# Two layers of a hybrid trunk on one core: ends of mixer branches moved behind the next projection, the softmax scaled by pairs of heads on VectorE, low priority for filler work only inside the triangular inverse

## The chip, the cores and the metric

One core of a Trainium2 chip runs one program. The metric is its device time in microseconds (us), median of several runs. The engines of the core have a queue of instructions each and work through it strictly in order: TensorE (PE in the profile; its weight loads are shown apart as PEld), VectorE (DVE), ScalarE (ACT) and GpSimd (POOL). SyncE (SP) issues the transfers of weights. An instruction waits on semaphores until the tiles that it reads are written and the tile that it overwrites is free.

## The reference

Two layers, 256 tokens, width 1024, in f32. Each layer adds the sum of four token mixers to its input and normalises, then does the same with a mixture of experts. What matters here, cut short:

```python
proj = x @ w_proj                                 # one wide input projection
y_a = _mla_branch(...)     # low-rank attention, 8 heads, causal softmax
y_b = _gla_branch(...)     # gated linear attention, chunks of 64
y_c = _gdn_branch(...)     # gated delta rule: conv of 4 taps on q, k, v, chunked, triangular solve
y_d = _rwkv7_branch(...)   # RWKV-7 state update
# attention inside _mla_branch:
s = jnp.where(key_pos[None, :] <= q_pos[:, None], s, -jnp.inf)
p = jax.nn.softmax(s, axis=-1)
o = einsum('bhqk,bkhd->bqhd', p, v)
# end of _gla_branch and of _gdn_branch, per head of 128 channels:
o = _rmsnorm(o, norm_g) * jax.nn.silu(gate)
# merge and output projection:
merged = sum(sigmoid(gate_logits[:, :, n]) * (y_n @ w_branch[n]) for n in range(4))
mix = merged @ w_out
x = _layernorm(alpha * x + mix)
x = _layernorm(alpha * x + moe(x))                # 16 experts, top 2
```

## The kernel before

All weights are streamed: a load brings 512 KB as a tile `raw` (128x1024, f32), ScalarE rounds it to a high half `hi` (L285, `split_hi`) and VectorE subtracts to get the low half `lo` (L289, `split_lo`). Each product is then three matmuls (Xh by hi, Xl by hi, Xh by lo). One call of `proj(i)` makes 256 columns of the input projection for all 256 tokens in a PSUM bank tagged "pp": two loads, 48 matmuls of 128x128 by 128x256. The banks have three tags: "pp" (two banks) for projections, "pc" (four) and "pf" (two) for the work inside the branches.

The four branches are written one after the other, and each interleaves its own chain (transposes, small matmuls, VectorE and ScalarE work) with the calls of `proj` for its inputs. A scheduler orders the instructions of each engine when the program is built; code that is written earlier or has a higher priority is taken first. While a branch works on a chain without projections of its own, `gap(us)` issues some microseconds of filler work: pieces of `merge(n, y)`, which project a finished branch and its gate. Fillers run at a low priority (`tc.high_priority(offset=-LOW)`), and the next matmul of the branch is put behind the last of them.

The places that the change touches:

- Attention in the MLA branch handles two groups of four heads (`hg`). For each, ScalarE makes eight exponentials (L914, L916: for each head a block `me0` of 128 queries by 128 keys and a block `me1` of 128 by 256), with the row sums in `sms`. VectorE takes the reciprocal of all sums (L918), GpSimd multiplies `me0` (L919) and `me1` (L920), and TensorE transposes them (by a multiplication with the constant `ident`, shown as `con`) for the product with v.
- `headnorm_T` ends both the gated linear attention (`gla`) and the delta rule (`gdn`): squares, sums, a power of -0.5 on GpSimd (`rsqrt`, L632), the product `hon` (L962), and a function `post()` that transposes `hon` on TensorE and multiplies by the gate into `y`. `gla` calls both its `post()` after a `gap`; `gdn` calls that of the second chunk after a `gap`.
- `gdn` convolves q, k and v on VectorE into `gacc` (L992, L1010); for v four transposes of `gacc` follow at once. In its chunk step, `gr` is scaled on VectorE (L1099) and subtracted from v on GpSimd (L1100).
- The output projection makes two halves (`hf`) of the columns in two banks tagged "pp" each. The last two banks of that tag were those of `merge_last`, emptied into `gth` (L626). `out_mm` (L1549 to L1551) multiplies the merged tile `mg`.

`rLT` is a tile of the RWKV branch that GpSimd sets to zero ahead of use (L1390).

## Time and profile before

| what | value |
|---|---|
| median of 3 runs | 1575.59 us (1574.55 to 1580.73) |
| profiled execution, its own time | 1570.59 us |
| span of its instructions | 1568.7 us |
| mean granted TensorE clock | 0.969 |
| TensorE busy | 1444.0 us, 92% |
| VectorE busy | 1147.0 us, 73% |
| ScalarE busy | 878.3 us, 56% |
| GpSimd busy | 178.6 us, 11% |

The span runs from the first to the last instruction; 1.9 us of the execution's time lie outside of it. The profiled execution is one run, and 5.0 us faster than the median of the others. Busy shares are averages over stages: the mixers of the two layers lie at 20 to 475 and 795 to 1255 us, the experts at 485 to 775 and 1265 to 1555 us.

### The profile page before, as it was taken

The page shows a single profiled execution, that of the slowest core. Times are in us where ns is not written, and L with a number is a line of the kernel's source. Part 1 is how long each engine was busy: PE and PEld are TensorE (multiplying, and loading weights), DVE is VectorE, ACT ScalarE, POOL GpSimd, SP SyncE. Part 2 cuts the span into 40 slices and gives each one's busy share as a digit, 9 for nine tenths or more (in the row PEclk, how much of TensorE's full clock was granted, in tenths as well). Part 3 has the DMA queues.
Part 4 walks back from the last instruction along what each step waited for, and adds up shares of the span by engine and source line. Part 5 has one row for each costly group of instructions (what it writes and reads, how often), then busy time and mean ns, then how long its engine had stood idle before and what let it go on. Part 6 is the DMA issues. An engine that isn't in the chain of part 4 may idle for free. (4 is left out here: it accounts for less than half of the span.)

```text
span 1568.7 us, 26671 instructions
## 1 busy us (share of the span) xinstructions
PE 1444.0 (92%) x10266; PEld 1155.3 (74%) x10266; DVE 1147.0 (73%) x1843; ACT 878.3 (56%) x1379; POOL 178.6 (11%) x203
## 2 busy tenths in 40 slices
PE   6999999899996999999789999997999979999995
PEld 6789989799985656654378899896999756665552
DVE  5567768883668988879656577678745689888795
ACT  4445445444347878776453563453333488787762
POOL 2111103211200000000011111232211000000000
PEclk8999999999998999999989999998999989999998
DMA  5434444363555899999633345343636468999992
GB/s 203 138 104 135 139 142 130 114 201 116 202 178 218 308 329 361 356 342 363 220 116 121 115 149 155 98 155 92 185 123 227 149 243 303 339 353 357 352 367 99
DMA packets 111446, 329.30 MB, mean 210 GB/s; under 512 B 29008, under 2 KB 31824, under 8 KB 111312
## 3 DMA queue, kind: packets, MB, share of 16 engines
q1 hardware_dynamic: 111312, 327.52, 60.4%
q8 instruction: 84, 1.38, 0.3%
q14 instruction: 50, 0.41, 0.1%
HBM read 322.63 MB, written 3.80 MB: 208 GB/s over the span
## 5 line engine op out<-in xcount | busy, mean ns | idle before, releaser
L289 DVE TENSOR_TENSOR lo<-raw,hi 128x1024 fp32r<-128x1024 f32 x476 | 584.5, 1249 | 114.9 <-ACT hi L285 106.7
L285 ACT CAST hi<-raw 128x1024 fp32r<-128x1024 f32 x476 | 486.9, 1047 | 303.0 <-PE pp L498 124.0
L504 PE MATMUL pp<-Xh,hi 128*128 128x256 f32 x736 | 216.4, 294 | 6.7 <-ACT hi L285 4.1
L504 PE MATMUL pp<-Xh,lo 128*128 128x256 f32 x736 | 214.8, 292 | 3.4 <-DVE lo L289 3.3
L504 PE MATMUL pp<-Xl,hi 128*128 128x256 f32 x736 | 213.8, 290 | 0.0
L504 PEld LDWEIGHTS pp<-Xh,hi 128*128 128x128 f32 x736 | 145.3, 197 | 9.8 <-ACT hi L285 4.7
L498 PE MATMUL pp<-Xh,hi 128*128 128x256 f32 x512 | 148.3, 291 | 3.0 <-ACT gth L574 3.0
L2020 PE MATMUL s<-whole,hT 128*64 128x512 f32 x336 | 150.2, 596 | 0.0
L504 PEld LDWEIGHTS pp<-Xh,lo 128*128 128x128 f32 x736 | 145.1, 197 | 4.4 <-DVE lo L289 3.8
L504 PEld LDWEIGHTS pp<-Xl,hi 128*128 128x128 f32 x736 | 145.1, 197 | 0.6 <-issue 0.2
L498 PE MATMUL pp<-Xl,hi 128*128 128x256 f32 x512 | 145.2, 285 | 0.0
L498 PE MATMUL pp<-Xh,lo 128*128 128x256 f32 x512 | 144.6, 284 | 0.0
L2020 PEld LDWEIGHTS s<-whole,hT 128*64 128x64 f32 x336 | 43.7, 137 | 93.5 <-issue 88.4
L1979 PE MATMUL u<-lo,r 128*128 128x512 f32 x256 | 103.1, 403 | 8.3 <-DVE lo L289 8.0
L1979 PE MATMUL g<-lo,r 128*128 128x512 f32 x256 | 102.5, 400 | 3.3 <-DVE lo L289 3.1
L1978 PE MATMUL g<-hi,r 128*128 128x512 f32 x256 | 103.8, 406 | 0.0
L498 PEld LDWEIGHTS pp<-Xh,hi 128*128 128x128 f32 x512 | 97.7, 191 | 6.4 <-ACT gth L574 3.4
L1978 PE MATMUL u<-hi,r 128*128 128x512 f32 x256 | 101.0, 394 | 0.0
L498 PEld LDWEIGHTS pp<-Xl,hi 128*128 128x128 f32 x512 | 97.9, 192 | 0.8 <-issue 0.6
L498 PEld LDWEIGHTS pp<-Xh,lo 128*128 128x128 f32 x512 | 97.9, 192 | 0.7 <-issue 0.6
L2026 ACT CAST Y<-s 64x512 fp32r<-64x512 f32 x60 | 34.8, 580 | 72.6 <-PE s L2020 72.6
L1979 PEld LDWEIGHTS u<-lo,r 128*128 128x128 f32 x256 | 48.0, 188 | 28.6 <-DVE lo L289 19.5
(563 smaller groups left out, 2795.3 us busy)
## 6 DMA issues: line engine op xcount, KB each, us to landing
raw<-win SPq DMA_DIRECT2D x156, 512.0 KB, 3.7
raw<-wg SPq DMA_DIRECT2D x122, 512.0 KB, 7.1
raw<-wu SPq DMA_DIRECT2D x120, 512.0 KB, 5.1
whole<-wd SPq DMA_DIRECT2D x92, 512.0 KB, 7.4
raw<-wd SPq DMA_DIRECT2D x36, 512.0 KB, 6.0
raw<-wbr SPq DMA_DIRECT2D x32, 512.0 KB, 4.0
raw<-wout SPq DMA_DIRECT2D x16, 512.0 KB, 4.7
whole<-wu SPq DMA_DIRECT2D x8, 512.0 KB, 5.1
```

Of the source, the lines that this page charges most:

```text
L285: done["hi"] = S.copy(hi, src).ins
L289: done["lo"] = V.tensor_tensor(lo, src, hi.bitcast(F32), OP.subtract).ins
L498: last[0] = f(*args, **kw).ins
L504: f(*args, **kw)
L1978: PE.matmul(x["p"], xs, hi[:, 512 * k2:512 * (k2 + 1)], start=(k == 0), stop=False)
L1979: PE.matmul(x["p"], xs, lo[:, 512 * k2:512 * (k2 + 1)], start=False, stop=(k == 7))
L2020: PE.matmul(py, x["hT"][:, f - NSP, :], w[:, cs], start=(f == 0), stop=(f == 3))
L2026: S.copy(Y[0:64, cs], py)
```

## The change

Five edits:

1. The softmax's reciprocal and its two multiplications go by pairs of heads, inside the loop that transposes, and the multiplications are done on VectorE.
2. The end of `gla` (both `post()`), the end of `gdn` (the second chunk's `post()`) and the transposes of v in `gdn` are not issued where they were, but put on a list `pending`; `settle()`, called right after the next `proj`, issues them. The `gap`s ahead of both ends are gone.
3. In the delta rule's chunk step VectorE subtracts `gr` instead of GpSimd.
4. The output projection's first half uses two banks tagged "pc".
5. `gap` takes its priority as an argument: fillers are low only in the triangular inverse, and elsewhere have the normal priority.

(`fr` frees a tile's slot.)

```diff
-        def gap(us):
+        def gap(us, low=0):
...
-                    with tc.high_priority(offset=-LOW):
+                    with tc.high_priority(offset=-low):
...
-                gap(GT / len(LTs))
+                gap(GT / len(LTs), LOW)
...
-                V.reciprocal(sm0, sm0)
-                G.tensor_tensor(e0, e0, bcast(sm0[:, 0, :], 128), OP.mult)
-                G.tensor_tensor(e1, e1, bcast(sm0[:, 1, :], T), OP.mult)
                 a0 = al([128, 4, T], "ma0")
                 a1 = al([128, 4, 128], "ma1")
                 for j in range(2):
+                    js = slice(2 * j, 2 * j + 2)
+                    V.reciprocal(sm0[:, :, js], sm0[:, :, js])
+                    V.tensor_tensor(e0[:, js, :], e0[:, js, :], bcast(sm0[:, 0, js], 128), OP.mult)
+                    V.tensor_tensor(e1[:, js, :], e1[:, js, :], bcast(sm0[:, 1, js], T), OP.mult)
                     p = bank(bk).rearrange("p (h k) -> p h k", h=2)
...
                 p = proj(2 + j)
+                settle()
                 pin = al([128, 2, T], "gpin")
...
                     V.scalar_tensor_tensor(acc, th, 1.0, acc, op0=OP.add, op1=OP.mult)
-                    pt = bank(bk).rearrange("p (c a d) -> p c a d", c=2, a=2)
-                    for a in range(2):
-                        for c in range(2):
-                            tp(pt[:, c, a, :], acc[:, a, 128 * c:128 * (c + 1)], ident)
-                    S.activation(vtok[:, :, 2 * g:2 * g + 2, :], pt, AF.Copy, scale=0.5)
+                    fr(th, pin)
+
+                    def turn_v(acc=acc, g=g):
+                        pt = bank(bk).rearrange("p (c a d) -> p c a d", c=2, a=2)
+                        for a in range(2):
+                            for c in range(2):
+                                tp(pt[:, c, a, :], acc[:, a, 128 * c:128 * (c + 1)], ident)
+                        S.activation(vtok[:, :, 2 * g:2 * g + 2, :], pt, AF.Copy, scale=0.5)
+                        fr(acc)
+
+                    pending.append(turn_v)
+                    continue
                 fr(acc, th, pin)
             for j in range(2):
                 p = proj(8 + j)
+                settle()
...
-            G.tensor_tensor(r1, vtok[:, 1], r1, OP.subtract)
+            V.tensor_tensor(r1, vtok[:, 1], r1, OP.subtract)
...
             post1 = headnorm_T(qs, rqk[:, 1, :], 1, gdnnh, zs, y)
-            gap(G4)
-            post1()
-            fr(qs, zs)
+            fr(qs)
+
+            def end():
+                post1()
+                fr(zs)
+
+            pending.append(end)
...
+        pending = []
+
+        def settle():
+            while pending:
+                pending.pop(0)()
...
-            yield 0.0
-            gap(G4)
-            for f in posts:
-                f()
-            fr(E1, E2, vt, og, at, St)
+            fr(E1, E2, at, St)
+
+            def end():
+                for f in posts:
+                    f()
+                fr(vt, og)
+
+            pending.append(end)
...
             p = proj(10)
+            settle()
...
         for hf in range(2):
-            pb = [bank("pp") for _ in range(2)]
+            pb = [bank("pp" if hf else "pc") for _ in range(2)]
```

What the scheduler makes of it on TensorE, at three places.

TensorE at the first pair of the first head group (`pp_...` are projections, `con_63` the identity): before, the two halves of the group start with both `me0`, late in projection `pp_761`.

```order
L504 MATMUL pp_761<-Xh_131,lo_795 128x256
L504 MATMUL pp_761<-Xh_131,hi_794 128x256
L504 MATMUL pc_496<-con_63,me0_480 128x128
L504 MATMUL pc_502<-con_63,me0_480 128x128
L504 MATMUL pp_761<-Xl_132,hi_794 128x256
L504 MATMUL pp_761<-Xh_131,lo_795 128x256
L504 MATMUL pp_761<-Xh_131,hi_794 128x256
L504 MATMUL pp_761<-Xl_132,hi_794 128x256
L504 MATMUL pp_761<-Xh_131,lo_795 128x256
L504 MATMUL pc_496<-con_63,me1_481 128x128
```

The same place after, from the first transpose on (the projection is now numbered `pp_767`).

```order
L504 MATMUL pp_767<-Xh_131,hi_770 128x256
L504 MATMUL pc_496<-con_63,me0_480 128x128
L504 MATMUL pp_767<-Xl_132,hi_770 128x256
L504 MATMUL pp_767<-Xh_131,lo_771 128x256
L504 MATMUL pp_767<-Xh_131,hi_770 128x256
L504 MATMUL pp_767<-Xl_132,hi_770 128x256
L504 MATMUL pc_496<-con_63,me1_481 128x128
L504 MATMUL pc_496<-con_63,me0_480 128x128
L504 MATMUL pc_496<-con_63,me1_481 128x128
L504 MATMUL pp_767<-Xh_131,lo_771 128x256
L504 MATMUL pp_767<-Xh_131,hi_800 128x256
```

The first pair's four transposes stand 18 projection matmuls further ahead than the first did before, and the second pair's follow nine matmuls later.

TensorE at the end of the gated linear attention, before (projection `pp_1105` of the delta rule goes on around it).

```order
L504 MATMUL pp_1105<-Xl_132,hi_1108 128x256
L504 MATMUL pp_1105<-Xh_131,lo_1109 128x256
L504 MATMUL pc_1087<-con_63,hon_1070 128x128 x4
L504 MATMUL pp_1105<-Xh_131,hi_1108 128x256
L504 MATMUL pp_1105<-Xl_132,hi_1108 128x256
```

And after.

```order
L504 MATMUL pp_1099<-Xl_132,hi_1132 128x256
L504 MATMUL pp_1099<-Xh_131,lo_1133 128x256
L504 MATMUL pc_1160<-con_63,hon_1076 128x128 x4
L504 MATMUL pc_1166<-con_63,hon_1091 128x128 x4
L504 MATMUL pp_1195<-Xh_131,hi_1198 128x256
```

Before, the first four stood 3 matmuls into that projection and the second four, not shown, 19 matmuls later; after, both stand at its end, behind all of its matmuls.

TensorE at the output projection of layer 0, before.

```order
L1549 MATMUL pp_5033<-hi_5037,mg_5014 128x512
L1550 MATMUL pp_5033<-lo_5038,mg_5014 128x512
L1549 MATMUL pp_5034<-hi_5037,mg_5014 128x512
L1550 MATMUL pp_5034<-lo_5038,mg_5014 128x512
L1551 MATMUL pp_5033<-hi_5037,mg_5017 128x512
```

And after (`mg_5020` is the same high half as `mg_5014`, `mg_5023` the same low half as `mg_5017`).

```order
L1574 MATMUL pc_5039<-hi_5043,mg_5020 128x512
L1575 MATMUL pc_5039<-lo_5044,mg_5020 128x512
L1574 MATMUL pc_5040<-hi_5043,mg_5020 128x512
L1575 MATMUL pc_5040<-lo_5044,mg_5020 128x512
L1574 MATMUL pp_5139<-hi_5143,mg_5020 128x512
L1574 MATMUL pp_5140<-hi_5143,mg_5020 128x512
L1576 MATMUL pc_5039<-hi_5043,mg_5023 128x512
```

The first half's four matmuls go to two "pc" banks; ahead of the first that needs the low half stand now two of the second half, in the "pp" banks.

## Rows read from the trace of the kernel before

**Rows 1.** Totals of the page: busy us (share of the span) and instructions by engine.

```profile
PE 1444.0 (92%) x10266; PEld 1155.3 (74%) x10266; DVE 1147.0 (73%) x1843; ACT 878.3 (56%) x1379; POOL 178.6 (11%) x203
```

**Rows 2.** TensorE's waits: for which tile; us in total, times, longest.

```profile
PE pc L504 <- DVE hon L962: 7.4, 8, 1.4
PE pc L504 <- POOL me L920: 6.3, 4, 1.8
...
PE pf L504 <- DVE gacc L1010: 5.2, 2, 2.7
...
PE pp L1549 <- DVE gth L626: 4.1, 2, 2.6
...
PE pc L504 <- POOL gr L1100: 1.9, 2, 0.9
...
PE pc L504 <- POOL me L919: 1.5, 4, 0.5
```

**Rows 3.** Windows: mixers, then MoE of layer 0; busy us (x instructions) by engine.

```profile
20.00:475.00 455.00, 430.09 (x3900) 398.76 (x3898) 300.89 (x547) 206.75 (x345) 76.39 (x84) 0.98 0.45 143
485.00:775.00 290.00, 281.74 (x1186) 170.61 (x1185) 245.81 (x305) 218.68 (x323) 7.03 (x9) 0.99 0.90 330
```

**Rows 4.** Timeline, attention's first head group: start us, us, engine, ..., [idle before, releaser].

```profile
69.43 0.21 ACT L916 ACTIVATION_READ_ACCUMULATOR me<-pc,mxs,rq 128x1 f32 x1
...
71.39 0.23 ACT L916 ACTIVATION_READ_ACCUMULATOR me<-pc,mxs,rq 128x1 f32 x1
...
72.58 4.30 DVE L289 TENSOR_TENSOR lo<-raw,hi 128x1024 fp32r<-128x1024 f32 x2 [0.73 <-ACT hi L285]
...
73.03 0.44 PE L504 MATMUL pc<-con,me 128*128 128x128 f32 x2 [0.34 <-POOL me L919]
...
73.66 0.28 PE L504 MATMUL pp<-Xl,hi 128*128 128x256 f32 x1
...
73.78 0.28 PE L504 MATMUL pp<-Xh,lo 128*128 128x256 f32 x1
...
75.86 1.31 PE L504 MATMUL pc<-con,me 128*128 128x128 f32 x10 [1.80 <-POOL me L920]
```

**Rows 5.** Line L920 on its own: durations in ns, min/median/max.

```profile
L920 POOL TENSOR_TENSOR me<-me,sms x4: 1895/2874/2876, 72.9 to 866.7; 128x1024 f32<-128x1024 f32 x4
```

**Rows 6.** VectorE's groups by shape: busy us, mean ns of one.

```profile
L289 DVE TENSOR_TENSOR lo<-raw,hi 128x1024 fp32r<-128x1024 f32 x476 | 584.5, 1249 | 114.9 <-ACT hi L285 106.7 <-PE g L1979 3.3 <-issue 1.4
...
L1459 DVE TENSOR_TENSOR ryt<-pc,rst 128x256 f32<-128x256 f32 x8 | 3.4, 424 | 0.2
...
L918 DVE RECIPROCAL sms<-sms 128x8 f32<-128x8 f32 x4 | 0.8, 204 | 10.7 <-ACT me L916 10.7
```

**Rows 7.** Timeline, end of the gated linear attention.

```profile
115.92 0.66 PE L504 MATMUL pc<-con,hon 128*128 128x128 f32 x4 [1.25 <-DVE hon L962]
...
118.56 0.69 DVE L962 TENSOR_TENSOR hon<-pc,hst 128x512 f32<-128x512 f32 x1 [0.93 <-POOL hst L632]
...
119.40 0.63 PE L504 MATMUL pc<-con,hon 128*128 128x128 f32 x4 [0.56 <-DVE hon L962]
```

**Rows 8.** Timeline of VectorE ahead of gacc.

```profile
154.14 0.17 DVE L1028 TENSOR_SCALAR grq<-gs 128x8 f32<-128x8 f32 x1 [3.10 <-POOL gs L632]
```

**Rows 9.** Delta rule's second chunk: timeline (two rows), memset rLT by line.

```profile
232.92 1.26 POOL L1100 TENSOR_TENSOR gr<-gvt,gr 128x512 f32<-128x512 f32 x1 [2.77 <-DVE hst L955]
...
245.49 0.63 PE L504 MATMUL pc<-con,hon 128*128 128x128 f32 x4 [1.36 <-DVE hon L962]
...
L1390 POOL MEMSET rLT<- 128x1024 f32 x4 | 3.8, 955 | 7.2 <-DVE rBK L1362 4.2 <-DVE rv L1313 1.3 <-DMA raw<-win 1.2
```

**Rows 10.** Timeline of TensorE at the first output projection.

```profile
446.30 0.50 PE L1549 MATMUL pp<-hi,mg 128*128 128x512 f32 x1 [1.54 <-DVE gth L626]
...
447.24 0.39 PE L1549 MATMUL pp<-hi,mg 128*128 128x512 f32 x1
447.47 0.39 PE L1550 MATMUL pp<-lo,mg 128*128 128x512 f32 x1
```

More of the change, by code (lines that the diff above doesn't have):

```diff
@@ L704, in tri_inv @@
                         S.copy(Dl[r, :, r], Dc[r, 0])
-                gap(GT / len(LTs))
+                gap(GT / len(LTs), LOW)
             P1s = []
@@ L715, in tri_inv @@
                 P1s.append(P1)
-                gap(GT / len(LTs))
+                gap(GT / len(LTs), LOW)
             for P1, Dc, Dt, Dl in zip(P1s, Dcs, Dts, Dls):
@@ L728, in tri_inv @@
                 fr(P1, Dc)
-                gap(GT / len(LTs))
+                gap(GT / len(LTs), LOW)
             Q1s = []
@@ L738, in tri_inv @@
                 Q1s.append(Q1)
-                gap(GT / len(LTs))
+                gap(GT / len(LTs), LOW)
             for Q1, Dt in zip(Q1s, Dts):
@@ L745, in tri_inv @@
                 fr(Q1)
-                gap(GT / len(LTs))
+                gap(GT / len(LTs), LOW)
             return Dts
```

## The prediction

> **What bounds the kernel now.** I read the page's totals first. TensorE is busy for 1444.0 us of a span of 1568.7 us [rows 1], so the time can fall only where TensorE stands still, or where its work is slower than it need be. The windows by stage come next: in the mixers of layer 0 TensorE is busy 430.09 of 455 us and in the following MoE 281.74 of 290 us [rows 3]. The MoE is nearly full whenever it starts, so a microsecond saved in the mixers moves everything behind it forward, and since both layers run the same code each saving counts twice. Then I read TensorE's waits, because each names the tile that was late [rows 2]. Six of them are what the edits touch: the head-normalised tile hon 7.4 us in 8 waits, the softmax tiles me 6.3 us in 4 (L920) and 1.5 us in 4 (L919), gacc 5.2 us in 2, the gate tile gth behind which the first output matmuls stand 4.1 us in 2, and gr 1.9 us in 2. Together they are 26.4 us.
>
> A wait's row is a little smaller than what the wait costs. Two matmuls in a stream start 0.12 us apart (73.66 and 73.78) although each is shown for 0.28 us [rows 4]. The transpose that waited for me started at 75.86, that is 2.08 us after the last matmul where 0.12 us would have been normal, so it cost 1.96 us and its row says 1.80. The difference, 0.16 us, is added to each wait. For 22 waits it makes 3.5 us, and the ceiling of all edits is 30 us.
>
> **The change part by part.**
>
> *Softmax scaling.* Now, per group of four heads, VectorE takes one reciprocal when all eight exponentials are done, then GpSimd multiplies me0 (L919) and me1 (L920, mostly 2.87 us [rows 5]), and TensorE waits for both [rows 4]. For four groups the two rows of waits plus 8 times 0.16 make 7.8 + 1.3 = 9.1 us. In the changed order the work goes by pairs: reciprocal (0.20 us), a multiplication of 128x256 and one of 128x512, on VectorE. Rows of those shapes take 0.42 and 0.69 us [rows 6, 7], so a pair costs 1.31 us and a group 2.6 us, where VectorE spent 0.2. The first pair's last exponential ends at 69.64 and the second's at 71.62 [rows 4], so me0 of the first pair is ready near 69.64 + 0.20 + 0.42 = 70.3 and its me1 at 71.0; the second pair's are ready at 72.2 and 72.9. TensorE used to arrive at 73.03 - 0.34 - 0.16 = 72.53 [rows 4], with 18 more matmuls of the projection ahead than now; it will arrive 18 x 0.12 = 2.2 us earlier, at 70.3 to 70.4. Four matmuls further, at 70.9, it needs me1 (a wait of some 0.1 us). Nine matmuls and some transposes after that, near 72.4, it needs the second pair (0.1 to 0.5 us). I leave 0.4 us of waiting in each group, 1.6 us in all: **gain 7.5 us**. The bounds: 9.1 us if no wait stays, about 4 us if each group keeps one wait of 1.3 us, the length of one pair's work.
>
> Those 2.4 us per group are added to a queue that also makes the weights' low halves, so I looked at what VectorE did beside GpSimd. Two of these splits took 4.30 us from 72.58, while L920 ran [rows 4], and one takes 1.25 us on average [rows 6]: GpSimd's multiplication cost VectorE 1.8 us of its own time. VectorE's real addition is therefore 2.4 - 1.8 = 0.6 us per group, and its idle time ahead of the reciprocal covers that. The Trainium skill (Perfetto Trace Analysis, Optimizing Scalar/DVE Operations) warns that shifting work between GpSimd and VectorE might not help, as the two share a read port. The row bears out the sharing: what GpSimd gives up, VectorE gets back. If the port were all that counts, this edit would gain nothing and the sum would be 4.75 us; I hold the order to count, since TensorE waits for me's time of completion and not for VectorE's total, and the scaling by pairs can start 2 us before the last exponential.
>
> *End of the gated linear attention.* The two sets of hon transposes stood 3 and 22 matmuls into a projection; now both stand behind its 39 further matmuls. They waited 1.25 and 0.56 us [rows 7], so 1.41 + 0.72 = 2.13 us with the correction. The second hon was made from 118.56 on in 0.69 us [rows 7], so it is ready near 119.25. TensorE began the second set at 119.40; without the two waits, without the first set's 0.4 us of transposes and with 17 more matmuls ahead it comes to the first set at 119.40 - 2.13 - 0.4 + 17 x 0.12 = 118.9 and to the second at 119.3. Nothing is left of the wait, or 0.1 us of it: **gain 2.1 us a layer, 4.2 us**. What ends later is y, and its consumer is a merge that is only issued much further on.
>
> *Transposes of v in the delta rule.* The diff puts them behind the next projection, but TensorE already ran them there: they stood 9 and 3 matmuls behind it before and the order is unchanged. What is late is gacc, because VectorE's queue is held for 3.10 us at L1028 until GpSimd's power of a 128x16 tile is done [rows 8], and the convolution that makes gacc is queued behind. The changed program has the same instructions in the same order there. **Gain 0**; the other bound is the whole wait, 5.2 + 0.3 = 5.5 us.
>
> *Delta rule, second chunk.* The subtraction that makes gr moves from GpSimd, where it ended at 234.18 after 1.26 us [rows 9], to VectorE at 0.69 us [rows 7]. There a token shift and a small product now stand ahead of it, some 0.4 us by my estimate, so about 0.2 us is won. Against this, in layer 0 the memset of rLT (0.96 us [rows 9]) now waits for that subtraction and stands in GpSimd's queue ahead of the power that the first hon needs; VectorE's L962 waits for the power, and u, hon and a scan are queued behind it. That makes hon some 0.9 us later, and 14 projection matmuls (1.7 us) that now precede it on TensorE about cover this. The second hon, with its wait of 1.36 us [rows 9], is now behind a projection, but only 34 matmuls stand between the two where 43 stood, so TensorE comes 1.1 us earlier to a tile whose chain has one split (1.25 us) in front of it now instead of one in the middle. I take +0.2 us a layer lost, **-0.4 us**. The bounds: 1.52 us lost again per layer (the second wait doubles), or the two waits for hon gone, 2 x 1.1 us net gained.
>
> *Output projection.* The first half's accumulators no longer need the bank that gth (L626) holds up to 446.30 [rows 10]. Four matmuls go ahead in them, but then come the second half's first two, in the old banks, and the second of these waits for the same gth. At 446.30 TensorE resumes as before, and the next after that needs a low half of mg that comes no sooner than before; it is two matmuls further by then, 0.23 us each (447.24 to 447.47 [rows 10]): **gain 0.5 us a layer, 0.95 us**. The bounds are 0 and the whole wait, 4.1 + 0.3 = 4.4 us.
>
> *Priority.* Outside the triangular inverse the filler matmuls have normal priority. In layer 0 TensorE's order isn't changed by it; in layer 1 a few groups of five to twenty-four matmuls change places in the RWKV part. **0**, with 1 us either way.
>
> **The sum.** 7.5 + 4.2 + 0 - 0.4 + 0.95 + 0 = 12.25 us, 0.8%. The profiled execution took 1570.59 us and would take 1558.3. The median of the runs shown is 1575.59 us, 5.0 us more than the profiled one; carried over, the prediction is 1563.3 us.
>
> **Rivals.**
> *All six waits go:* 30 us less, 1546 us. It needs VectorE's hold at L1028 to end, and no row or order shows why it should. 7%. A part of it, the gacc wait alone going, would give 1558.
> *The waits only change their name:* each pair of heads keeps a wait of about 1.3 us, the second hon doubles its wait, the output gains nothing. That is 12.25 - 3.5 - 2.6 - 0.95 = 5 us gained, 1570 us, within what can't be told from no change (0.5% of 1575.59 is 7.9 us, and I take that as the limit of this measurement). For it speaks how small the margins above are (0.1 us at several places), against it that TensorE reaches them behind other work. With the softmax's whole gain lost, as by the Trainium skill's warning above, it would be 1571. 25%.
> *Slower:* VectorE's queue becomes the limit in attention. Its six instructions of a group stand together, so a split of weights behind them can be held from 69.64 to 72.9, 3.3 us. If TensorE needs that split each time, four groups cost 13.2 us instead of gaining 7.5, and the kernel takes 1563.3 + 20.7 = 1584 us. It decides once splits are made less than 3.3 us before use. Against it: the two splits beside L920 ended at 76.88, and TensorE still waited only for me. 10%.
> My forecast, 1557 to 1568 us, has 58%.
>
> **How the numbers follow.** Faster by over 0.5% means under 1567.7 us: nearly all of the forecast, the 7%, and little of the second rival: 0.63. Within 0.5%: 0.28. Slower: 0.09. The range runs from 1554 (all waits of softmax, hon and output gone, or gacc's too) to 1577 us (the second rival with its spread).
>
> **What would show it.** Right: in the profile after, the rows for me and for hon of the gated linear attention are gone or under 0.5 us each; gacc's wait still shows about 2.6 us twice; the output still waits for gth, by the four matmuls' time less; VectorE's busy time grows by less than 10 us and the splits beside the softmax take 1.25 us again. Wrong: a new wait of TensorE for a low half around the attention, a hon wait above 1.5 us in the delta rule, or a new order in layer 1's RWKV part that waits longer than before.

## The result, and the profile after

The changed kernel takes 1559.73 us (median of 4 runs, 1556.61 to 1562.93), the kernel before 1575.07 us beside it (4 runs, 1573.76 to 1580.73). The ratio is 0.9895 with a 95% interval of 0.9867 to 0.9923: about 1.0% faster. The profiled executions took 1570.59 and 1557.93 us, their spans differ by 1568.7 - 1556.0 = 12.7 us; the prediction was 12.25 us for them.

The page's totals after, to be read beside [rows 1]. TensorE has the same instructions; it is busy for 1.3 us less and stands still for 11.4 us less.

```profile
span 1556.0 us, 26689 instructions
...
PE 1442.7 (93%) x10266; PEld 1155.7 (74%) x10266; DVE 1148.4 (74%) x1865; ACT 877.1 (56%) x1379; POOL 159.2 (10%) x193
```

TensorE's waits after (for which tile; us in total, times, longest), beside [rows 2]:

```profile
PE pf L504 <- DVE gacc L1013: 5.2, 2, 2.7
...
PE pc L504 <- DVE hon L964: 4.1, 4, 1.3
...
PE pp L1574 <- DVE gth L627: 1.8, 2, 1.4
...
PE pp L1574 <- ACT hi L285: 1.2, 1, 1.2
...
PE pc L504 <- DVE hst L959: 0.8, 2, 0.4
```

Both rows for me and the row for gr are gone, and hon is down from 8 waits with 7.4 us to 4 with 4.1 us, all of them in the delta rule. The wait for gacc is exactly what it was. The output still waits for gth, 1.8 instead of 4.1 us, and has a new wait beside it, for a high half of weights. In place of gr stands a small one for hst, at the same matmul: 0.42 us in each layer where 0.94 stood.

To see what each stage gained I took the starts of the input projections' matmuls out of the traces (they come in the same number in every kernel) and measured stages between two of them: attention from the 193rd to the 385th, the end of the gated linear attention (GLA) to the 433rd, the transposes of v from the 673rd to the 721st, the delta rule's chunks from the 865th to the 1105th. In layer 1 the stages start at the 2017th, 2257th, 2545th and 2737th and hold the same matmuls, except that attention has 48 more there, ahead of the softmax. In us, worked out so from the traces (layer 0 / layer 1):

| kernel | attention | end of GLA | v | chunks |
|---|---|---|---|---|
| before | 40.97 / 55.05 | 12.84 / 12.84 | 10.36 / 9.09 | 57.08 / 56.70 |
| changed | 35.89 / 51.95 | 10.66 / 10.65 | 10.35 / 10.43 | 56.48 / 56.76 |
| mla_only | 35.88 / 52.06 | 12.84 / 12.84 | 10.19 / 10.58 | 58.97 / 60.34 |
| pool_pairs | 37.54 / 53.20 | 10.66 / 10.65 | 10.39 / 10.59 | 57.02 / 57.64 |
| dve_whole | 35.95 / 51.24 | 10.65 / 10.65 | 10.34 / 9.11 | 57.12 / 57.19 |
| gacc_fix | 35.88 / 51.87 | 10.66 / 10.66 | 6.19 / 6.19 | 57.20 / 55.44 |
| gr_pool | 35.92 / 51.86 | 10.66 / 10.66 | 8.86 / 9.09 | 57.92 / 57.91 |
| gdn_now | 35.92 / 51.90 | 10.66 / 10.66 | 10.33 / 9.09 | 55.73 / 55.79 |

So attention gained 5.1 and 3.1 us, the end of the gated linear attention 2.18 and 2.19, the chunks 0.6 and nothing; the stage of v lost 1.3 us in layer 1. That is 11.8 of the 12.7 us. What lies outside these stages nearly cancels: 1.5 us gained ahead of the first attention and 2.0 us in layer 0 behind the chunks (the output projection apart), against 0.6 and 1.5 us lost in the two output projections and 1.1 us between the chunks and the output projection of layer 1.

The 3.1 us of layer 1 are too small a figure for the softmax. From the 2065th matmul on, the counterpart of layer 0's 193rd, attention took 40.31 us before and 35.73 in the changed kernel, both at full clock: 4.6 us gained. The 48 matmuls ahead of it took 1.5 us longer, with a new wait of 0.4 us (for kh) and 4.0 instead of 1.7 us at TensorE's lower clock.

Part of the scatter is TensorE's clock: a stage in which it was granted the lower of its two levels, 1.2 instead of 2.4 GHz, for 3.4 us is up to 1.7 us longer. In the stage of v it shows best: 8.86 to 9.1 us without such a stretch, 10.2 to 10.6 with one. Both figures of mla_only's chunks hold one too.

The timeline after of the first head group (start us, us, engine, line, ...), VectorE and then TensorE, beside [rows 4]:

```profile
68.17 0.18 DVE L923 RECIPROCAL sms<-sms 128x4 f32<-128x4 f32 x1 [0.41 <-ACT me L917]
68.38 0.43 DVE L924 TENSOR_TENSOR me<-me,sms 128x256 f32<-128x256 f32 x1
68.73 0.68 DVE L925 TENSOR_TENSOR me<-me,sms 128x512 f32<-128x512 f32 x1
70.14 0.18 DVE L923 RECIPROCAL sms<-sms 128x4 f32<-128x4 f32 x1 [0.73 <-ACT me L917]
70.36 0.42 DVE L924 TENSOR_TENSOR me<-me,sms 128x256 f32<-128x256 f32 x1
70.70 0.68 DVE L925 TENSOR_TENSOR me<-me,sms 128x512 f32<-128x512 f32 x1
71.68 1.23 DVE L289 TENSOR_TENSOR lo<-raw,hi 128x1024 fp32r<-128x1024 f32 x1 [0.29 <-ACT hi L285]
...
68.95 0.30 PE L504 MATMUL pc<-con,me 128*128 128x128 f32 x1
...
69.57 0.51 PE L504 MATMUL pc<-con,me 128*128 128x128 f32 x3
...
70.98 0.49 PE L504 MATMUL pc<-con,me 128*128 128x128 f32 x3
```

VectorE takes 0.18, 0.43 and 0.68 us for a pair, close to the prices read from other lines [rows 6, 7]. The last pair's me1 is done at 71.4, 1.3 us after its last exponential, where GpSimd was done 4.2 us after it. None of TensorE's rows carries a wait, and the next split, at 71.68, takes 1.23 us again.

The end of the gated linear attention on TensorE, beside [rows 7]: all eight transposes in one go, with no wait ahead.

```profile
112.26 1.04 PE L504 MATMUL pc<-con,hon 128*128 128x128 f32 x8
```

The second chunk of the delta rule: VectorE's subtraction, GpSimd, TensorE's two sets of transposes, beside [rows 9].

```profile
224.59 0.68 DVE L1111 TENSOR_TENSOR gr<-gvt,gr 128x512 f32<-128x512 f32 x1
...
225.33 0.95 POOL L1415 MEMSET rLT<- 128x1024 f32 x1 [3.82 <-DVE gr L1111]
226.36 1.26 POOL L633 TENSOR_TENSOR hst<-hst,con 128x4 f32<-128x4 f32 x1
...
229.16 0.63 PE L504 MATMUL pc<-con,hon 128*128 128x128 f32 x4 [0.95 <-DVE hon L964]
...
236.81 0.66 PE L504 MATMUL pc<-con,hon 128*128 128x128 f32 x4 [1.17 <-DVE hon L964]
```

The subtraction ends at 225.27, the memset of rLT starts on it and the power only behind the memset, as the prediction had it. The first hon now costs 0.95 us of waiting instead of 0.54, and the second 1.17 instead of 1.36 (layer 1: 0.70 instead of 0.54, 1.27 instead of 1.37).

### The profile page after: what moved, and what is told of

Same layout as the page of the kernel before. It is cut to its first block, busy times and chain, and to the rows that moved or that the text cites. A ratio compares the mean times of both kernels' runs of the same rounds, so it can differ in the third digit from the quotient of the medians.

```text
span 1556.0 us, 26689 instructions
## 1 busy us (share of the span) xinstructions
PE 1442.7 (93%) x10266; PEld 1155.7 (74%) x10266; DVE 1148.4 (74%) x1865; ACT 877.1 (56%) x1379; POOL 159.2 (10%) x193
## 5 line engine op out<-in xcount | busy, mean ns | idle before, releaser
L289 DVE TENSOR_TENSOR lo<-raw,hi 128x1024 fp32r<-128x1024 f32 x476 | 578.7, 1236 | 118.1 <-ACT hi L285 109.6
```

Source lines behind the costliest of these rows:

```text
L289: done["lo"] = V.tensor_tensor(lo, src, hi.bitcast(F32), OP.subtract).ins
```

## The experiments

A ratio to the kernel before is given where a kernel ran several times. The others (out_pp, out_pin, out_fix, out_only, gr_pool, gdn_now) have one execution each, from 1556.6 to 1580.13 us, and of them only stages are compared, as the kernel before took up to 1592.28 us beside them.

**mla_only.** The kernel before with the first edit.

```diff
-                V.reciprocal(sm0, sm0)
-                G.tensor_tensor(e0, e0, bcast(sm0[:, 0, :], 128), OP.mult)
-                G.tensor_tensor(e1, e1, bcast(sm0[:, 1, :], T), OP.mult)
                 for j in range(2):
+                    js = slice(2 * j, 2 * j + 2)
+                    V.reciprocal(sm0[:, :, js], sm0[:, :, js])
+                    V.tensor_tensor(e0[:, js, :], e0[:, js, :], bcast(sm0[:, 0, js], 128), OP.mult)
+                    V.tensor_tensor(e1[:, js, :], e1[:, js, :], bcast(sm0[:, 1, js], T), OP.mult)
```

> The kernel before with edit 1 alone (softmax scaled by pairs on VectorE). Theory: the softmax edit by itself gives two thirds of the whole gain, since the time that matmul progress gained between attention's start and end was 5.1 and 4.9 us in the changed kernel; so 8 to 10 us less than before (ratio near 0.994), no wait for me left in TensorE's rows. Rival, that the shared port decides and shifting work between GpSimd and VectorE gives nothing: within 2 us of before, with new waits for a low half beside the attention.

Ratio 0.9952 (0.9926 to 0.9978), 7.6 us by that (3.5 to 11.7), just under the expected 8 to 10. Attention is as short as in the changed kernel (35.88 and 52.06 us; 35.83 from the 2065th matmul on), 9.6 us less than before in the two layers, and no wait for me is left, so the edit does its whole work alone. The 9 runs lie far apart (1560.95 to 1575.9 us) and go with the mean granted clock (0.971 and 0.959), which makes the ratio the blunter of the two measures.

**pool_pairs and dve_whole.** The changed kernel with one half of the first edit each: pairs, but on GpSimd; VectorE, but the whole group at once.

```diff
-                    V.tensor_tensor(e0[:, js, :], e0[:, js, :], bcast(sm0[:, 0, js], 128), OP.mult)
-                    V.tensor_tensor(e1[:, js, :], e1[:, js, :], bcast(sm0[:, 1, js], T), OP.mult)
+                    G.tensor_tensor(e0[:, js, :], e0[:, js, :], bcast(sm0[:, 0, js], 128), OP.mult)
+                    G.tensor_tensor(e1[:, js, :], e1[:, js, :], bcast(sm0[:, 1, js], T), OP.mult)
...
+                V.reciprocal(sm0, sm0)
+                V.tensor_tensor(e0, e0, bcast(sm0[:, 0, :], 128), OP.mult)
+                V.tensor_tensor(e1, e1, bcast(sm0[:, 1, :], T), OP.mult)
```

> The changed kernel with the scaling still by pairs, but both multiplications on GpSimd. Theory: the pairs let the first transposes start early, but a pair on GpSimd costs about half of 1.04 + 1.9 to 2.9 us, 1.5 to 2 us after the pair's reciprocal, and VectorE's splits beside it are stretched again; the second pair is ready some 0.7 to 1 us later than on VectorE, so a wait of 0.5 to 1 us stays in each of the four groups: 2 to 4 us slower than the changed kernel. Rival, that the pairs alone are the gain and the engine is indifferent: within 1 us of the changed kernel.

> The changed kernel with one reciprocal and two multiplications for a whole head group, on VectorE. Theory: the engine matters more than the pairs, because me1 of a whole group takes 1.25 us on VectorE where GpSimd took 2.87: all is ready about 2.1 us after the last exponential, some 2 us earlier than before the change and 0.8 us later than by pairs; a wait of 0 to 1 us for me1 stays per group, so 1 to 4 us slower than the changed kernel. Rival, that the pairs are the gain: nearly the whole 10 us are lost again.

Pairs on GpSimd: ratio 0.9906 (0.9875 to 0.9938), which can't be told from the changed kernel's. Attention takes 37.54 us in layer 0, 1.65 more than in the changed kernel, and 1.3 more in layer 1, 3.0 in all, as expected (2 to 4); small waits are back. The rows are TensorE's waits, then GpSimd's me1 of the first pair:

```profile
PE pc L504 <- POOL me L925: 1.3, 3, 0.4
...
PE pc L504 <- POOL me L924: 0.3, 1, 0.3
...
68.12 1.04 POOL L925 TENSOR_TENSOR me<-me,sms 128x512 f32<-128x512 f32 x1
```

The whole group on VectorE: ratio 0.9892 (0.9862 to 0.9922), attention 35.95 and 51.24 us. The 51.24 look shorter than the changed kernel's 51.95 only because the 48 matmuls ahead ran at a higher clock; from the 2065th matmul on it is 36.45 against 35.73. So it loses 0.8 us in the two layers by this measure, and the times show none of it: less than the 1 to 4 us that I expected. VectorE, then TensorE, of that kernel's first group:

```profile
68.64 0.20 DVE L919 RECIPROCAL sms<-sms 128x8 f32<-128x8 f32 x1 [2.39 <-ACT me L917]
68.88 0.69 DVE L920 TENSOR_TENSOR me<-me,sms 128x512 f32<-128x512 f32 x1
69.49 1.22 DVE L921 TENSOR_TENSOR me<-me,sms 128x1024 f32<-128x1024 f32 x1
70.62 2.35 DVE L289 TENSOR_TENSOR lo<-raw,hi 128x1024 fp32r<-128x1024 f32 x2
...
69.71 0.41 PE L504 MATMUL pc<-con,me 128*128 128x128 f32 x2
...
70.92 1.25 PE L504 MATMUL pc<-con,me 128*128 128x128 f32 x10
```

The whole scaling is done at 70.71, 2.1 us after the last exponential, and TensorE starts the first transposes at 69.71 without a wait: the scheduler put the projection's matmuls ahead of them. The four combinations side by side, in us of attention (layer 0 / layer 1 from the 2065th matmul on, all at full clock):

| scaled on | whole group | by pairs |
|---|---|---|
| GpSimd | 40.97 / 40.31 (before) | 37.54 / 37.04 (pool_pairs) |
| VectorE | 35.95 / 36.45 (dve_whole) | 35.89 / 35.73 (changed) |

Each half of the edit takes most of the wait away by itself: pairs on GpSimd gain 3.3 to 3.4 us a layer, VectorE with whole groups 3.9 to 5.0. Once VectorE scales, pairs add nothing in layer 0 and 0.7 us in layer 1; with pairs, VectorE adds 1.3 to 1.7.

**gacc_fix.** The changed kernel with three small instructions moved.

```diff
-                    V.scalar_tensor_tensor(acc, th, 1.0, acc, op0=OP.add, op1=OP.mult)
+                    vlast = V.scalar_tensor_tensor(acc, th, 1.0, acc, op0=OP.add, op1=OP.mult).ins
+                    if j == 4:
+                        v4 = vlast
...
-            V.tensor_scalar(rqk, s8[:, :, 0:4], 128.0 ** -0.5, None, op0=OP.mult)
+            with tc.issue_after(v4):
+                V.tensor_scalar(rqk, s8[:, :, 0:4], 128.0 ** -0.5, None, op0=OP.mult)
```

(The same `with` stands ahead of `ikn` and of the first `rho`.)

> The changed kernel with three small instructions of VectorE (grq, gikn and the first of grho, which read the power that GpSimd makes in 2.9 us) put behind the gacc of the first v block in VectorE's queue, so that the convolution isn't held for them. TensorE's order is the same there. Theory: the wait for gacc (5.2 us in 2) goes, and with it the stretch at the lower clock that follows each of them in the changed kernel's records (near 151 and 916 us): 5 to 8 us faster than the changed kernel. Rival, that gacc is late because VectorE has too much to do there: the wait stays at 2 us or more each and the time within 2 us.

Ratio 0.9857 (0.9826 to 0.9889), 1553.66 us. The stage of v is 4.2 us shorter in both layers (6.19 us), the wait for gacc has no row any more. VectorE and TensorE there:

```profile
142.87 0.18 DVE L1037 TENSOR_SCALAR gstat<-pc 128x16 f32<-128x16 f32 x1 [0.44 <-PE pc L504]
142.96 2.45 DVE L995 SCALAR_TENSOR_TENSOR gacc<-gpin,vec,gacc 128x255 f32<-128x255 f32 x6
145.33 1.22 DVE L289 TENSOR_TENSOR lo<-raw,hi 128x1024 fp32r<-128x1024 f32 x1
146.46 0.69 DVE L1013 SCALAR_TENSOR_TENSOR gacc<-gth,gacc 128x512 f32<-128x512 f32 x1
147.06 0.17 DVE L1042 TENSOR_SCALAR grq<-gs 128x8 f32<-128x8 f32 x1
...
147.92 0.60 PE L504 MATMUL pf<-con,gacc 128*128 128x128 f32 x4
```

The convolution (L995) starts 0.1 us behind gstat instead of 3.4 us behind it, and grq comes when the power is done. The hold at that line was the cause. The two stages of v are 8.4 us shorter than in the changed kernel, 5.2 us by the waits and the rest by the stretches at the lower clock, which are gone too. The spans differ by 5.8 us, and the ratio to the changed kernel's is 0.9857 / 0.9895 = 0.996, 6 us: within the expected 5 to 8. The intervals of the two ratios overlap, but none of the 4 runs (1552.0 to 1555.62 us) is as long as the shortest of the changed kernel (1556.61).

**out_pp, out_pin, out_fix, out_only.** Edit 4 undone; edit 4 with the second half held behind the first; the same with mg's splits at high priority; the kernel before with edit 4 alone.

```diff
-            pb = [bank("pp" if hf else "pc") for _ in range(2)]
+            pb = [bank("pp") for _ in range(2)]
...
-                PE.matmul(pb, yh, wh, start=(k == 0), stop=False)
+                if hf and k == 0:
+                    with tc.issue_after(olast[0]):
+                        PE.matmul(pb, yh, wh, start=True, stop=False)
+                else:
+                    PE.matmul(pb, yh, wh, start=(k == 0), stop=False)
...
         for kp in range(4):
-            ysplit(merged[:, 2 * kp:2 * kp + 2, :], mhl[0][kp], mhl[1][kp], 0.5)
+            with tc.high_priority():
+                ysplit(merged[:, 2 * kp:2 * kp + 2, :], mhl[0][kp], mhl[1][kp], 0.5)
```

> The changed kernel with edit 4 undone (the output projection's first half in the old banks). In the changed kernel the same count of output matmuls ran at the same distance from the kernel before (9.8 us in layer 0) ahead of the projection and behind it, so the edit seems to have gained nothing. Theory: the next thing late is the low half of mg, which VectorE makes behind the same gth; so undoing it changes the end of the first half by less than 0.3 us in layer 0, and in layer 1 the 1.2 us wait for a high half of the second half's weights goes away without making that stage faster by more than what a stretch at the lower clock there took (1 us). Rival, my recorded term: the stage gets 0.5 us longer in each layer.

> The changed kernel with the second half's matmuls held behind the first half's last one, so that TensorE doesn't run into the bank of gth. Theory: TensorE's wait for gth (1.8 us in 2) becomes a wait for mg's low half of the same end, and the stage is as long as in the changed kernel within 0.3 us (in layer 1 less whatever the lower clock took there). Rival: the order was at fault, and without it the first half starts 1.4 us earlier in each layer.

> As the run before, and the splits of mg issued with high priority, so that VectorE makes the first two low halves ahead of the last gth instead of behind it. Theory: with the low half early the first half of the output runs without a stop: 1.5 to 2 us gained in each layer against the changed kernel, no wait for gth or mg above 0.5 us. Rival: another piece of the same chain, the low half of the weights, stops it as long.

> The kernel before with edit 4 alone (the output projection's first half in the other banks). From the last matmul of the last merge to the first transposes behind the first half it took 13.07 us before in layer 0 and 14.17 in layer 1, at full clock in both. Theory: edit 4 gains nothing, 13.0 to 13.6 and 14.0 to 15.4 us, since a low half of mg comes next; where the stage shows a stretch at the lower clock it is up to 1.7 us more. Rival, my recorded term: 12.6 and 13.7 us.

From the last matmul of the merge to the first transposes behind the first half, in us (a star marks a stretch at the lower clock in that stage):

| kernel | layer 0 | layer 1 |
|---|---|---|
| before | 13.07 | 14.17 |
| mla_only (without edit 4) | 14.05 | 14.25 |
| out_only | 13.39 | 16.41* |
| pool_pairs (has edit 4) | 13.09 | 17.04* |
| changed | 13.63 | 15.67* |
| gr_pool (has edit 4) | 13.06 | 15.34 |
| out_pp | 14.92* | 15.72* |
| out_pin | 15.62* | 16.88* |
| out_fix | 14.94 | 15.36* |

At full clock the stage takes 13.06 to 13.63 us with edit 4 in layer 0, out_fix apart, 13.07 and 14.05 without. By itself that would not rule out a gain of 0.5 us, but the rows inside the stage do. The first half can't end before VectorE has made a low half of mg. In the kernel before and in pool_pairs (with edit 4) the last gth starts on VectorE 1.42 us behind the first output matmul alike. The first output matmul, the first that needs a low half and the first transposes, before and then in pool_pairs:

```profile
444.14 0.40 PE L1549 MATMUL pp<-hi,mg 128*128 128x512 f32 x1
...
446.90 0.50 PE L1551 MATMUL pp<-hi,mg 128*128 128x512 f32 x1
...
457.20 0.60 PE L1560 MATMUL pf<-con,xt 128*128 128x128 f32 x4
```

```profile
436.59 0.40 PE L1574 MATMUL pc<-hi,mg 128*128 128x512 f32 x1
...
439.34 0.50 PE L1576 MATMUL pc<-hi,mg 128*128 128x512 f32 x1
...
449.67 0.49 PE L1585 MATMUL pf<-con,xt 128*128 128x128 f32 x3
```

The low half is used after 2.76 and 2.75 us, and the transposes follow 10.30 and 10.33 us later. Those 10.3 us are the same in every stage at full clock but out_fix's, with edit 4 or without (10.30 to 10.33 in eleven stages); with a stretch at the lower clock they are 11.4 to 11.9, out_fix again apart. So edit 4 moves nothing that counts. What makes whole stages longer at full clock lies elsewhere: VectorE's queue standing further back (changed, layer 0), or a wait ahead of the first output matmul (mla_only 0.6 us for gth in layer 0, gr_pool 0.9 us for a high half of mg in layer 1). The changed kernel's rows, VectorE first, then TensorE:

```profile
436.23 0.68 DVE L627 SCALAR_TENSOR_TENSOR gth<-gth,pp 128x512 f32<-128x512 f32 x1
436.83 0.68 DVE L558 SCALAR_TENSOR_TENSOR mg<-merged,mg 128x512 fp32r<-128x512 f32 x1
...
436.97 0.49 PE L1574 MATMUL pp<-hi,mg 128*128 128x512 f32 x1 [1.37 <-DVE gth L627]
437.57 0.50 PE L1576 MATMUL pc<-hi,mg 128*128 128x512 f32 x1
```

TensorE gets its bank at 436.97, does one matmul, and needs the low half of mg, which VectorE makes from 436.83 to 437.51: gth's bank and mg's low half come out of the same queue, one behind the other. With the second half held back (out_pin) the same delay stands at mg:

```profile
PE pc L1582 <- DVE mg L558: 5.4, 2, 2.7
```

5.4 us in 2 for mg, where the changed kernel has 1.8 for gth and 1.2 for weights. My repair (out_fix) failed: mg's splits came ahead of the last gth, but behind a split of weights, and TensorE waited 4.9 us in 3 for them. A rival of the recorded kind held: another piece of the same chain.

Against the other expectations: out_only's stages are as expected (up to 1.7 us more with a stretch at the lower clock). In out_pp layer 0 is 1.3 us longer than in the changed kernel, not within 0.3, and in out_pin 2.0 us; both have a stretch at the lower clock there. The three kernels that have the other edits without edit 4 (out_pp, combo2, combo3) all show such a stretch in layer 0, of the nine with edit 4 gdn_now and out_pin do. Whether edit 4 has to do with that is open.

**gr_pool and gdn_now.** The changed kernel with edit 3 undone; with the end of the delta rule issued where it was.

```diff
-            V.tensor_tensor(r1, vtok[:, 1], r1, OP.subtract)
+            G.tensor_tensor(r1, vtok[:, 1], r1, OP.subtract)
...
-            def end():
-                post1()
-                fr(zs)
-
-            pending.append(end)
+            gap(G4)
+            post1()
+            fr(zs)
```

> The changed kernel with edit 3 undone (gr subtracted on GpSimd again). Theory: in layer 0 the wait for gr comes back with 0.9 us, and the first hon of the chunk comes back earlier, since the memset of rLT no longer stands ahead of its power; so the stage from the transposes of gacc to the second hon is 0 to 1 us longer than in the changed kernel in each layer. Rival, my recorded term of -0.2 us a layer: it gets 0.2 us shorter.

> The changed kernel with the delta rule's end issued where it was (behind filler work, not behind the next projection); edit 3 stays. The stage from the first projection of the decay to the RWKV part took 57.1 and 56.7 us before, 56.5 and 56.8 with all edits, 57.9 and 57.9 with edit 3 undone. Theory: edit 3 gains 1.2 us a layer and moving the end loses 0.6 to 1.2, so here the stage takes 55.4 to 56.0 us in each layer. Rival: the end's move is neutral and the stage takes 56.5 to 56.8 as with all edits.

The chunks take 57.92 and 57.91 us without edit 3, 55.73 and 55.79 us with it and without the moved end, and 56.48 and 56.76 us with both. So in this comparison edit 3 gains 1.2 to 1.4 us a layer and moving the end costs 0.75 to 1.0 us, gdn_now as expected, gr_pool a little above its 0 to 1 us (two matmuls more lie in its stage of layer 0). But other kernels with both edits took 55.4 to 57.6 us at full clock (out_pp, the same program up to this point, 57.3 and 57.1), so neither figure is clear of the scatter. Of the single waits, gr's came back in gr_pool with 0.94 us in each layer, where the changed kernel has 0.42, and the first hon's fell from 0.95 and 0.70 to 0.57 and 0.54.

**combo2 and combo3.** gacc_fix without edit 4, and this with the delta rule's end where it was.

> The changed kernel with the three small instructions moved behind gacc (6 us faster in its own run) and edit 4 undone. Theory: edit 4 gains nothing in layer 0 and costs about 1 us in layer 1, so 6 to 8 us faster than the changed kernel, ratio to the kernel before 0.984 to 0.986. Rival: edit 4 gains its 0.5 us a layer: no faster than the three instructions' move alone (0.9857).

> As the run before, and the delta rule's end where it was before. Theory: 1 to 2 us less than that run, 8 to 10 us less than the changed kernel, ratio to the kernel before 0.983 to 0.985. Rival: what is won in these stages is given back where the output weights' transfer ends a wait ahead of the output projection, and the ratio stays at 0.986.

1554.39 us (4 runs, ratio 0.987, 0.9814 to 0.9927) and 1554.34 us (6 runs, 0.9861, 0.9818 to 0.9905): neither is better than gacc_fix alone, and their stages show the gain of gdn_now in the chunks no more (56.19 and 57.05 us in combo3 against 56.62 and 57.09 in combo2). Both expectations failed, and both rivals named the ratio that came: no faster than gacc_fix, and 0.986. Their reasons are not borne out: that edit 4 gains something is answered by the 10.3 us above, and no run tests the transfer of the output weights. What the traces show is a stretch at the lower clock in layer 0's output projection, 15.2 and 14.9 us in combo2 and combo3 against 13.4 in gacc_fix. The changed kernel with the three instructions moved is the simplest of the best versions.

The fifth edit was not run by itself: with low priority everywhere the changed kernel's instructions stand in the same order on TensorE, VectorE, GpSimd and SyncE, and on ScalarE one changes places in each layer. So the new order in layer 1's RWKV part, which the prediction put down to it, comes from the other edits.

## Why the prediction was right

The sum, 12.25 us, met 12.7 us between the profiled executions. The medians differ by 15.3 us, with 12 to 21 us as the interval of the ratio, so the sum lies at its low end, and the median came out 3.6 us under the predicted 1563.3. Not all terms met what they stand for. The signs named in advance came: the rows for me and for the hon of the gated linear attention are gone, gacc's wait is still 5.2 us in 2, gth's is smaller, VectorE is busy for 1.4 us more, and no low half is waited for in attention.

*What bounds it* was right: TensorE's waits named the places, and what the mixers saved came out at the end (10.8 us ahead at the first g matmul of layer 0's experts and 10.7 at the last, 13.1 us ahead at the end of the second layer's experts, 12.7 us at the end).

*Softmax:* the mechanism held, the size was too small. I left 0.4 us of waiting in each group and got 7.5 us; nothing was left, and it is 5.1 us in layer 0 and 4.6 in layer 1, counted over the same matmuls. These 9.7 us are the 9.1 us that the rows of waits gave as the bound, and a little more. One reason in that step fell in part: that the scaling by pairs can start ahead of the last exponential is worth nothing in layer 0 and 0.7 us in layer 1 once VectorE does it, as dve_whole shows; it would have been worth 3.3 to 3.4 us a layer on GpSimd. The section of the Trainium skill that warned of moving work between GpSimd and VectorE (Perfetto Trace Analysis, Optimizing Scalar/DVE Operations) also says that breaking up instructions may let work complete sooner where ScalarE or VectorE isn't saturated but causes bubbles on another engine. The warning did not come true here, since VectorE with whole groups brought attention from 40.97 to 35.95 us. Breaking up on VectorE brought 0.06 and 0.7 us.

*Gated linear attention:* 2.1 us a layer predicted, 2.18 and 2.19 measured, and in mla_only, which lacks the edit, 12.84 us as before.

*Transposes of v:* 0 predicted and 0 found in layer 0; the cause given, the hold of VectorE's queue, is shown by gacc_fix. What I left out is the clock: in layer 1 a stretch at 1.2 GHz now follows this wait, which cost 1.3 us.

*Delta rule's chunk:* -0.2 us a layer predicted, +0.6 and -0.1 measured. The order of events came as told (memset, then power, then hon). By the waits, moving the subtraction was sized too small: the matmul that reads gr waits 0.42 instead of 0.94 us, 0.5 us gained where 0.2 stood. The first hon lost 0.4 and 0.2 us, so the matmuls put ahead of it did not quite cover the later tile, and the second gained 0.2 and 0.1 where a loss was forecast. That is 0.3 to 0.5 us a layer gained. What gr_pool and gdn_now add to it, about 1 us for each of the two moves, is not clear of the scatter.

*Output projection:* +0.5 us a layer predicted; the edit itself gained nothing, and the stage took 0.6 and 1.5 us longer. The step that failed is that being two matmuls further when the low half of mg arrives shortens the first half. Its first matmul with a low half already started 0.05 us behind the end of VectorE's row for mg before the change, so only an earlier mg could have helped. In layer 0 VectorE's queue reached that point 0.5 us later against TensorE than before. In layer 1 the wait for a high half of weights took the place of gth's without delaying the first low half (3.91 us behind the first output matmul, 3.85 before), and the 1.5 us are the stretch at the lower clock.

So the close agreement of the sums is in part luck. Attention came out 2.2 us better than its term, the chunks 1.0 and the gated linear attention 0.2; the output projection 3.0 us worse, the stage of v 1.3. No term stood for 2.5 us lost at two other places of layer 1 (ahead of its attention and behind its chunks) or for about 4 us gained elsewhere, most of it ahead of the first attention and in layer 0 behind the chunks. That rest was not traced to an edit; some of it is where stretches at the lower clock fell.

## What to carry to other kernels

Add up the waits that name a tile and ask of each what stands next in the same queue: where the tile can be made sooner (the softmax, by a faster engine or in pieces) the whole wait goes, where the next tile comes out of the same queue (the output projection) nothing goes. When an edit has two halves, run all four combinations: here either half alone took most of the wait away. Look for a small instruction that holds an in-order queue for a slow helper: moving three of them by a few places was worth 6 us here, over a third of what the five edits gave. When stages change by a microsecond, compare stages in the trace between the same instructions, and look at the granted clock of each before believing a difference.

## What the runs showed of the hardware

GpSimd's multiplication of 128x1024 took 1.9 us in one case and 2.87 in the others [rows 5], and two splits of VectorE beside it 4.30 us where 2 x 1.25 were normal [rows 4, 6]; the 1.8 us that they lost are about GpSimd's 1.9 us alone. One by one, the two splits took 1.47 and 2.91 us, and the first ended at 74.05, 1.75 us ahead of GpSimd's end at 75.80. So GpSimd's multiplication seems to have stood behind the first split, and the second split behind it: they took turns rather than slowed each other by a share. In the fourth case a split began 0.5 us before GpSimd's end and took 0.35 us longer than usual, while VectorE's copy out of PSUM ran beside GpSimd in its usual 0.69 us. GpSimd, then VectorE:

```profile
866.72 1.90 POOL L920 TENSOR_TENSOR me<-me,sms 128x1024 f32<-128x1024 f32 x1
...
867.51 0.69 DVE L1165 COPY lvt<-pf 128x512 f32<-128x512 f32 x1 [1.87 <-PE pf L504]
868.12 1.58 DVE L289 TENSOR_TENSOR lo<-raw,hi 128x1024 fp32r<-128x1024 f32 x1
```

TensorE's clock does not fall behind every wait, and not only behind waits. After the 2.5 us wait for gacc in layer 0 it does (windows of the changed kernel; the third last column is the granted clock), while the same wait in layer 1 of the kernel before was followed by none (9.09 us at full clock):

```profile
139.00:151.20 12.20, 9.74 (x81) 9.44 (x81) 7.76 (x17) 7.18 (x13) 3.48 (x3) 1.00 0.33 105
151.20:154.60 3.40, 3.40 (x18) 3.40 (x17) 3.15 (x9) 1.94 (x3) 0.10 (x1) 0.51 0.71 235
```

But in the profiled execution of pool_pairs it stayed at half for 27.3 us behind 20 us in which TensorE was busy for 19.3, and no wait longer than 0.7 us lies there:

```profile
1113.80:1133.80 20.00, 19.33 (x494) 18.16 (x493) 11.07 (x14) 7.28 (x12) 6.61 (x10) 1.00 0.53 150
1133.80:1161.10 27.30, 27.30 (x217) 24.43 (x216) 6.69 (x8) 6.12 (x10) 1.26 (x1) 0.50 0.21 67
1161.10:1171.10 10.00, 10.00 (x103) 9.53 (x102) 2.45 (x2) 4.34 (x7) 0.00 (x0) 1.00 0.50 157
```

By half of 27.3 us that stretch cost up to 13.7 us (an estimate), and this execution, 1577.85 us, is 12.4 us longer than the next of that kernel's five. Why it came is open; no experiment here was made for it.
